# Two encoder layers on one core: raw blocks of the first product chunks fetched between the plain chunks, FFN forms made in one paced chain, a quarter of the plain weights' low halves by subtraction, activations' low halves on VectorE

## The chip, the cores and the metric

The kernel runs on one core of a Trainium2 chip. The metric is the device time of one execution in microseconds (us). The profile is of one execution; TensorE is PE in it, VectorE DVE, ScalarE ACT, GpSimd POOL, SyncE SP. A name such as L508 is line 508 of the kernel before.

## The reference, cut to what matters

Two layers, 512 tokens of 1024 channels, all in float32. Each layer has an attention part with three branches, which the change leaves alone, and a gated FFN:

```python
for l in range(DEPTH):                       # DEPTH = 2
    ...                                      # attention, pooling, gates, output projection
    hf = rms_norm(x, ffn_norm_g[l])
    u = depthwise_conv(hf @ ffn_w_up[l], ffn_conv_w[l], ffn_conv_b[l])   # 1024 -> 2*2816, width 3
    u_gate, u_val = u[..., :D_FF], u[..., D_FF:]
    x = x + (jax.nn.silu(u_gate) * u_val) @ ffn_w_down[l]                # 2816 -> 1024
```

## The kernel before

**Three matmuls for one.** A float32 product is made of three of a rounded type: each operand is split into a high half (its rounded value) and a low half (the rest), and hi·hi, hi·lo and lo·hi are summed. So every weight and every activation must be split before TensorE can use it. In the profile `wh`, `wl` are the halves of a weight, `HH`, `HL` those of the activations held in the long-lived buffers, `ah`, `al` those in short-lived ones.

**The FFN.** The 2816 hidden columns are 22 chunks of 128. A chunk has two parts, gate and value. Chunks 0 to 5 are **plain**: a part is eight steps of three matmuls of 128x512 into one PSUM tile (`ps_acc`, `ps_ST`, `ps_AV` in turn). Its weight comes in two pieces of 128x512, called units here, so that the plain stretch of a layer uses 24 units, numbered 0 to 23 in order of use, each 12 matmuls long. Chunks 6 to 21 are **product** chunks: gate and value come from seven products of 256 columns (`FORMS`), made from four raw blocks of 128x512 and sums of them, and from sums and differences of the normed input. The "down" projection (`ps_mi`) of finished chunks is dealt between the products.

**Plain weights.** SyncE fetches raw weights in one stream (`w_dma`, L390) into slots: three of 128x1024 (`RAW`) for two units each, and eight of 128x512 (`ALONE`) for the product chunks' blocks. A fetch is issued when a slot of its kind comes free (`w_free`), and the stream is strictly in order. `w_split` makes the halves of a unit. For a unit of kind "u", which all plain FFN units are, `by_transfer` (L414 to L423) has ScalarE write the high half, ScalarE write its negative into the low half, and GpSimd issue a DMA that adds the raw weight to it (L421); the row is `wl<-raw`, a DMA_DIRECT2D on POOL. For kind "p" it is a subtraction on VectorE or GpSimd, whichever a table of expected finish times calls sooner (`pick`). Product blocks' halves are `fh` and `fl`, by transfer, or come from sums on VectorE.

`wnext` is called where TensorE is about to use a unit, and has units split up to `LA` = 3 ahead, or `LAF` = 6 when the unit used now, or the one six on, belongs to a product.

**The forms.** When the normalising factor `rbc` is known, `build_forms` writes the normed input (`hn`, eight tiles), sums of its pieces (`tt`, four steps of four), and splits these into the product operands `tf`: names "11", "12" from `hn`, "1", "2", "22", "3" from `tt`, each a ScalarE copy and a VectorE subtraction. There are three chains of such steps, all started together. This runs beside the plain chunks. There VectorE also scales each finished part (`u`), convolves it (two SCALAR_TENSOR_TENSOR, `a<-u,prm,a`), and multiplies gate and value (`a<-a,a`); ScalarE then writes the product's high half, and GpSimd subtracts for the low half (`HL<-a,HH` or `al<-a,ah`, `eng=G` in `convolve`).

**The order.** A planner with a clock of its own records the program: `at` puts a step on its calendar, `chain` runs steps in turn, `need` marks what TensorE uses next. The engines then run what was recorded in order, each its own queue, so a step that waits holds up whatever was recorded behind it on the same engine.

Of the kernel before, what the change touches and what calls it, by code (L numbers as in the profile page):

```python
# [19 lines left out]
T = 512  # L20
D = 1024
KC = D // P
# [17 lines left out]
MID = 5  # L40
PRE_A = 16
PRE_B = 8
LA, LAF = 3, 6
SIZES = (6, 5, 4, 4, 3)
PLACE = {1: 0, 2: 5, 3: 0}
KEEP = 2
FORMS = ("11", "12", "1", "22", "2", "4", "3")
SPOTS = ("22", "2", "4", "3")
END = object()
# [83 lines left out]
def _layer_units():  # L133

    r = [("p", wd) for wd in _widths()]
    for tok in _ffn():
        if tok[0] == "u":
            r += [("u", T)] * 2
        elif tok[0] == "f":
            r.append(tok)  # L140
        elif (tok[2] * SIZES[tok[1]] + tok[3]) % 4 == 0:
            r.append(("u" if tok[1] < len(SIZES) - 1 else "p", T))
    return r


def _stream():


    pieces, slots, units, alone = [], [], [], []
    for kind, *u in _layer_units() * L:  # L150
        if kind == "f":
            if u[1] == FORMS[0]:
                first = len(pieces)
                for _ in range(4):
                    pieces.append((len(slots), 0, T))
                    slots.append(T)
                    alone.append(True)
            units.append((u[1], first))
            continue
        if len(slots) <= KC or alone[-1] or slots[-1] + u[0] > 1024:  # L160
            slots.append(0)
            alone.append(False)
        pieces.append((len(slots) - 1, slots[-1], u[0]))
        slots[-1] += u[0]
        units.append((kind, len(pieces) - 1))
    return pieces, slots, units, alone
# [25 lines left out]
class Clock:  # L192
# [37 lines left out]
    def done(self, *key):  # L230
        self.ready[key] = self.fin + self.SEM
# [7 lines left out]
    def has(self, *keys):  # L239
        return all(self.ready.get(k, 1e9) <= self.now for k in keys)  # L240

    def chain(self, *steps, after=0.2):

        def go(n, source=None):
            if n == len(steps):
                return
            keys, fn = steps[n] if isinstance(steps[n], tuple) else ((), steps[n])
            late = [self.ready.get(k, self.now + 0.5) for k in keys]
            if late and max(late) > self.now:
                self.at(max(late) - self.now, lambda: go(n))  # L250
                return
            self.fin, self.source, self.last = self.now, source, None
            fn()
            source, self.source = self.last, None
            self.at(max(0.0, self.fin - self.now), lambda: go(n + 1, source))
        self.at(after, lambda: go(0))

    def drain(self):
# [63 lines left out]
def trunk(ctx: ExitStack, tc: tile.TileContext, x, w, prm, gb, cst, out):  # L322
# [3 lines left out]
    at, need, done, chain = ck.at, ck.need, ck.done, ck.chain  # L326
    V, A, G = Engine(ck, nc.vector, "DVE"), Engine(ck, nc.scalar, "ACT"), Engine(ck, nc.gpsimd, "Pool")
# [48 lines left out]
    def f(ap):  # L376
        return ap.bitcast(F32)


    pieces, swidth, units, alone = _stream()  # L380
# [43 lines left out]
    def w_split():  # L424
        j = st["split"]
        kind, pi = units[j]
        st["split"] += 1
        if kind not in "pu":
            w_form(j, kind, pi)
            return  # L430
        sl, off, wd = pieces[pi]
        w_until(sl)
        r = raws[sl][:, off:off + wd]
        hi, lo = halves[j] = pair(j)
        ck.fin = ck.now
# [11 lines left out]
        if pi + 1 == len(pieces) or pieces[pi + 1][0] > sl:  # L447
            w_free(sl)

    def w_form(j, form, pi):  # L450
# [47 lines left out]

    def wnext():
        j = st["use"]  # L500
        n = LAF if any(units[min(i, len(units) - 1)][0] not in "pu" for i in (j, j + LAF)) else LA
        w_ahead(j + n if j > LA else j)
        st["use"] += 1
        need(("w", j))
        return halves.pop(j)
# [161 lines left out]
    def layer(l, sq, xsrc):  # L667
# [918 lines left out]
        act = {}  # L1586
# [8 lines left out]
        def build_forms():  # L1595
# [10 lines left out]
            def normed(k):  # L1606
                hn[k] = slot("hn")[:, :T]
                V.scalar_tensor_tensor(hn[k], XM[:, k, :], col(PRM_FG + k), fin["rbc"][:, :T], ALU.mult, ALU.mult)
                done("hn", l, k)

            def sums(q):
                a, b = hn[2 * q], hn[2 * q + 1]
                t = tt[q] = (slot("tt")[:, :T], slot("tt")[:, :T])
                V.tensor_tensor(t[0][:, lo], a[:, hi], a[:, lo], ALU.subtract)
                V.tensor_tensor(t[1][:, lo], b[:, hi], a[:, hi], ALU.subtract)
                V.tensor_tensor(t[0][:, hi], b[:, hi], t[0][:, lo], ALU.subtract)
                V.tensor_tensor(t[1][:, hi], b[:, lo], t[0][:, hi], ALU.subtract)
                done("tt", l, q)
# [36 lines left out]
        def convolve(c, part, u):  # L1655
            ci = c + part * FC
            a = slot("a")
            steps = [
                lambda: A.activation(a[:, :T], u[:, :T], AF.Identity, bias=col(PRM_B + ci),
                                     scale=col(PRM_W1 + ci)),  # L1660
                lambda: V.scalar_tensor_tensor(a[:, 1:T], u[:, 0:T - 1], col(PRM_W0 + ci), a[:, 1:T],
                                               ALU.mult, ALU.add),
                lambda: V.scalar_tensor_tensor(a[:, 0:T - 1], u[:, 1:T], col(PRM_W2 + ci), a[:, 0:T - 1],
                                               ALU.mult, ALU.add)]
            if part == 0:
                def gate():
# [340 lines left out]
```

## Time and profile before

| what | value |
|---|---|
| time, median of 3 runs | 1579.79 us (1577.57 to 1582.62) |
| the profiled execution's time | 1578.39 us |
| its span in the trace | 1576.6 us |
| its mean granted TensorE clock | 0.997 |
| plain stretch of layer 0, 432.65 to 498.00: VectorE busy | 50.51 of 65.35 us |
| the same: ScalarE busy | 50.44 us |
| the same: GpSimd busy, and its instructions | 32.08 us, 30 |
| the same: mean busy share of the DMA engines | 0.85 |

How to read the rows: a row of the timeline gives start, duration, engine, line, operation, output<-inputs, and in brackets the engine's idle time ahead of it with what ended it. A row of waits gives total, count and the longest. A row of windows gives a stretch, its length, the busy time of PE, weight loads, DVE, ACT and POOL with the number of instructions that started in it, then the granted TensorE clock, the DMA share and GB/s. TensorE's matmuls overlap, so the distance between starts is what one costs, and not the duration shown. A DMA_DIRECT2D row on POOL is the issue of a transfer; its landing is in the DMA view.

### The profile page before, as it was taken

How to read it: one execution, taken by the hardware profiler on the slowest of the kernel's cores; microseconds unless marked ns; L12 is line 12 of the kernel's file. 1: busy time of each engine (PE TensorE's matmuls, PEld its weight loads, DVE VectorE, ACT ScalarE, POOL GpSimd, SP SyncE). 2: the span in 40 equal slices, each digit the busy share in tenths (PEclk: the TensorE clock that was granted, in tenths of full speed). 3: DMA queues.
4: the chain of work that ended last, by engine and by line, in shares of the span. 5: the costliest groups of instructions: out<-in, count | busy, mean ns of one | idle time of the engine just before them, and what ended most of it. 6: DMA issues, size and time to landing. Idle time of an engine off the chain costs nothing.

```text
span 1576.6 us, 23997 instructions
## 1 busy us (share of the span) xinstructions
PE 1548.2 (98%) x8193; PEld 1338.6 (85%) x8193; DVE 1111.4 (70%) x1816; ACT 1034.4 (66%) x1932; POOL 859.7 (55%) x868
## 2 busy tenths in 40 slices
PE   9999989999999999999999999899999999999999
PEld 8888878888877999998888888788888779999987
DVE  6867886875278777777656688778652877777774
ACT  5557776763478777777655587666535787777773
POOL 3974876854653433333588658668546443333333
PEclk9999999999999999999999999999999999999999
DMA  5432224324489887886535322343244798888853
GB/s 205 126 114 74 74 85 144 107 67 134 113 179 230 200 193 185 205 183 132 135 117 141 100 74 74 96 138 101 70 146 123 170 229 192 192 198 187 194 113 101
DMA packets 127563, 222.36 MB, mean 141 GB/s; under 512 B 29648, under 2 KB 51664, under 8 KB 127440
## 3 DMA queue, kind: packets, MB, share of 16 engines
q1 hardware_dynamic: 90864, 162.93, 33.2%
q0 software_dynamic: 31680, 57.69, 21.3%
q8 instruction: 64, 1.05, 0.3%
q10 hardware_dynamic: 4896, 0.21, 0.2%
q14 instruction: 59, 0.48, 0.1%
HBM read 149.41 MB, written 13.63 MB: 103 GB/s over the span
## 4 chain that ended last, share of the span: by engine, by line
PE 74%; DVE 13%; ACT 6%; issue 4%; POOL 2%; DMA 1%; SPq 0%; ACTq 0%; DVEq 0%; POOLq 0%
PE ps_acc L508 32%; PE ps_AV L508 14%; PE ps_ST L508 12%; PE ps_S L508 8%; PE ps_mi L508 8%; DVE a L294 2%; DVE XM L290 2%; ACT wh L283 1%; DVE wl L290 1%; DVE u L290 1%; DVE mgl L290 1%; ACT mgh L283 1%; DVE hn L294 1%; ACT fh L283 1%; DVE tf L290 1%
## 5 line engine op out<-in xcount | busy, mean ns | idle before, releaser
L290 POOL TENSOR_TENSOR wl<-raw,wh 128x512 fp32r<-128x512 f32 (+3 forms) x241 | 305.0, 1275 | 224.6 <-ACT wh L283 206.5
L283 ACT ACTIVATE wh<-raw 128x512 fp32r<-128x512 f32 (+2 forms) x457 | 269.2, 605 | 56.9 <-DVE raw L290 12.9
L421 POOL DMA_DIRECT2D wl<-raw x124 | 110.9, 919 | 290.3 <-ACT wl L283 106.0
L508 PE MATMUL ps_acc<-HH,wl 128*128 128x512 f32 x416 | 164.3, 395 | 6.2 <-DMA wl<-raw 6.2
L508 PE MATMUL ps_acc<-HH,wh 128*128 128x512 f32 x416 | 164.1, 394 | 3.4 <-DVE vm L290 2.9
L294 DVE SCALAR_TENSOR_TENSOR a<-u,prm,a 128x511 f32<-128x511 f32 x176 | 142.8, 811 | 32.2 <-ACT a L283 31.2
L508 PE MATMUL ps_acc<-HL,wh 128*128 128x512 f32 x416 | 163.5, 393 | 0.0
L421 POOL DMA_DIRECT2D fl<-raw x96 | 85.2, 887 | 105.7 <-ACT sx L283 47.0
L290 DVE TENSOR_TENSOR wl<-raw,wh 128x512 fp32r<-128x512 f32 (+2 forms) x93 | 92.4, 995 | 60.6 <-ACT wh L283 60.5
L283 ACT ACTIVATE a<-u,prm 128x512 f32<-128x512 f32 x88 | 71.5, 815 | 86.6 <-DVE u L290 86.2
L298 DVE TENSOR_REDUCE nm<-ps_S 128x1 fp32r<-128x512 f32 x128 | 87.6, 685 | 36.0 <-PE ps_S L508 34.8
L508 PEld LDWEIGHTS ps_acc<-HH,wl 128*128 128x128 f32 x416 | 78.8, 189 | 24.9 <-DMA wl<-raw 7.9
L508 PEld LDWEIGHTS ps_acc<-HH,wh 128*128 128x128 f32 x416 | 79.0, 190 | 19.8 <-issue 4.4
L508 PE MATMUL ps_AV<-tf,wh 128*128 128x256 f32 x512 | 94.8, 283 | 0.0
L508 PE MATMUL ps_acc<-tf,wh 128*128 128x256 f32 x512 | 94.4, 282 | 0.0
L508 PE MATMUL ps_ST<-tf,fh 128*128 128x256 f32 x512 | 94.2, 281 | 0.0
L508 PEld LDWEIGHTS ps_acc<-HL,wh 128*128 128x128 f32 x416 | 78.9, 190 | 16.3
L508 PEld LDWEIGHTS ps_acc<-tf,wh 128*128 128x128 f32 x512 | 83.9, 191 | 5.3
L508 PEld LDWEIGHTS ps_AV<-tf,wh 128*128 128x128 f32 x512 | 81.4, 190 | 2.6
L283 ACT ACTIVATE wl<-wh 128x512 fp32r<-128x512 f32 x124 | 78.5, 633 | 3.9
L508 PEld LDWEIGHTS ps_ST<-tf,fh 128*128 128x128 f32 x512 | 79.4, 190 | 0.0
L508 PE MATMUL ps_acc<-tf,wl 128*128 128x256 f32 x256 | 72.4, 283 | 0.0
(417 smaller groups left out, 4844.8 us busy)
## 6 DMA issues: line engine op xcount, KB each, us to landing
raw<-w SPq DMA_DIRECT2D x162, 512.0 KB, 3.7
raw<-w SPq DMA_DIRECT2D x136, 256.0 KB, 4.2
wl<-raw POOLq DMA_DIRECT2D x124, 256.0 KB, 4.3
fl<-raw POOLq DMA_DIRECT2D x96, 256.0 KB, 5.4
raw<-w SPq DMA_DIRECT2D x14, 384.0 KB, 3.0
XM<-x SPq DMA_DIRECT2D x16, 256.0 KB, 3.2
dtq<-tr SPq DMA_DIRECT2D x16, 192.0 KB, 1.9
dtk<-tr SPq DMA_DIRECT2D x16, 192.0 KB, 2.0
```

What stands on the lines that cost most here:

```text
L283: return self.eng.activation(out, in_, func, **k)
L290: return self.eng.tensor_tensor(out, *a)
L294: return self.eng.scalar_tensor_tensor(out, *a)
L298: return self.eng.tensor_reduce(out, in_, *a, **k)
L421: nc.gpsimd.dma_start(f(lo), r, accum_op=ALU.add)
L508: PE.matmul(o, lhsT=lhsT, rhs=rhs, start=start, stop=stop, skip_group_check=again)
```

## The change

Five edits, all in the FFN:

1. **Fetch order.** After each of the last eight of the twelve plain parts, one raw block of the first two product chunks is put into the stream of fetches (the "q" marks), instead of four in a row ahead of each of these chunks.
2. **Low halves.** The second unit of each value part becomes kind "p": six of the 24 plain units of a layer (units 3, 7, 11, 15, 19, 23) are split by subtraction. `pick` gives all of them to GpSimd. This takes six ScalarE copies and six accumulating DMAs out of each layer.
3. **Lookahead** is `LAP` = 4 where plain units are in use.
4. **Forms.** `hn` and `tt` steps alternate in one chain that starts no step sooner than 0.9 us after the last, and all cuts stand in one chain with 0.8 us, where two chains without a pace were.
5. **Activations.** From chunk 5 on, the low halves of activations are subtracted on VectorE, 17 per layer.

```diff
-LA, LAF = 3, 6
+LA, LAP, LAF = 3, 4, 6
+PACE_H, PACE_F = 0.9, 0.8
...
         if tok[0] == "u":
-            r += [("u", T)] * 2
+            r += [("u", T), ("p" if tok[2] else "u", T)] + [("q",)]
...
+    early, plain, fresh = [], 0, False
     for kind, *u in _layer_units() * L:
+        if kind == "q":
+            plain = (plain + 1) % (2 * SIZES[0])
+            if plain and plain >= 2 * SIZES[0] - 8:
+                early.append(len(slots))
+                slots.append(T)
+                alone.append(True)
+            continue
...
                 for _ in range(4):
+                    if early:
+                        pieces.append((early.pop(0), 0, T))
+                        continue
...
-        if len(slots) <= KC or alone[-1] or slots[-1] + u[0] > 1024:
+        if len(slots) <= KC or fresh or alone[-1] or slots[-1] + u[0] > 1024:
...
-            self.at(max(0.0, self.fin - self.now), lambda: go(n + 1, source))
+            self.at(max(pace, self.fin - self.now), lambda: go(n + 1, source))
...
-        n = LAF if any(units[min(i, len(units) - 1)][0] not in "pu" for i in (j, j + LAF)) else LA
+        kinds_ = [units[min(j + i, len(units) - 1)][0] for i in (0, LAP, LAF)]
+        n = LAF if any(k not in "pu" for k in kinds_) else LAP if "u" in kinds_[:2] else LA
...
-            chain(*[lambda k=k: normed(k) for k in range(KC)], *[lambda q=q: sums(q) for q in range(4)], after=0.0)
-            for names in (("11", "1", "2"), ("12", "22", "3")):
-                chain(*[z for name in names for q in range(4) for z in cut(name, q)], after=0.3)
+            chain(*[z for q in range(4) for z in (lambda q=q: normed(2 * q), lambda q=q: normed(2 * q + 1), lambda q=q: sums(q))],
+                  after=0.0, pace=PACE_H)
+            chain(*[z for name in ("11", "12", "1", "2", "22", "3") for q in range(4) for z in cut(name, q)], after=0.3, pace=PACE_F)
...
-            return steps + [([("gate", l, c)], prod), *split(ah, al, a[:, :T], eng=G), lambda: done("act", l, c)]
+            return steps + [([("gate", l, c)], prod), *split(ah, al, a[:, :T], eng=G if c < SIZES[0] - 1 else V), lambda: done("act", l, c)]
```

How it moves instructions is shown at three places of layer 0; layer 1 has the same pattern. TensorE's order is the same in both kernels. The numbers behind a name only tell buffers apart, and the lines of the changed kernel lie 13 or 14 further down.

The first place is SyncE's queue in the second half of the plain stretch. Before:

```order
L390 DMA raw_4842<-w 128x1024
L390 DMA raw_4905<-w 128x1024
L390 DMA raw_4969<-w 128x1024
L390 DMA raw_5026<-w 128x1024
L390 DMA raw_5083<-w 128x1024
L390 DMA raw_5085<-w 128x512
L390 DMA raw_5087<-w 128x512
L390 DMA raw_5089<-w 128x512
L390 DMA raw_5091<-w 128x512
L390 DMA raw_5161<-w 128x1024
```

The last plain chunk's fetch, raw_5083, is followed by the four blocks of the first product chunk. In the changed kernel the queue reads, from the fetch for units 8 and 9:

```order
L403 DMA raw_4625<-w 128x1024
L403 DMA raw_4627<-w 128x512
L403 DMA raw_4679<-w 128x1024
L403 DMA raw_4681<-w 128x512
L403 DMA raw_4759<-w 128x1024
L403 DMA raw_4761<-w 128x512
L403 DMA raw_4817<-w 128x1024
L403 DMA raw_4819<-w 128x512
```

The blocks of 128x512 now stand one by one behind the fetches of 128x1024.

The second place is GpSimd's queue in the middle of the plain stretch, units 10 to 17. Before (L421 issues a transfer, L290 is a subtraction):

```order
L421 DMA wl_4797<-raw_4706 128x512
L421 DMA wl_4825<-raw_4706 128x512
L421 DMA wl_4853<-raw_4791 128x512
L421 DMA wl_4883<-raw_4791 128x512
L290 TENSOR_TENSOR al_4693<-a_4691,ah_4692 128x512
L421 DMA wl_4917<-raw_4842 128x512
L290 TENSOR_TENSOR al_4822<-a_4820,ah_4821 128x512
L421 DMA wl_4944<-raw_4842 128x512
L421 DMA wl_4981<-raw_4905 128x512
L421 DMA wl_5007<-raw_4905 128x512
```

In the changed kernel the same units read:

```order
L434 DMA wl_4782<-raw_4679 128x512
L303 TENSOR_TENSOR wl_4835<-raw_4679,wh_4834 128x512
L434 DMA wl_4839<-raw_4759 128x512
L434 DMA wl_4870<-raw_4759 128x512
L434 DMA wl_4899<-raw_4817 128x512
L303 TENSOR_TENSOR al_4700<-a_4698,ah_4699 128x512
L303 TENSOR_TENSOR al_4832<-a_4830,ah_4831 128x512
L303 TENSOR_TENSOR wl_4953<-raw_4817,wh_4952 128x512
L434 DMA wl_4957<-raw_4879 128x512
L434 DMA wl_4996<-raw_4879 128x512
```

Two of the transfers, for units 11 and 15, are now subtractions on GpSimd itself, and the two `al` stand together behind unit 14's transfer.

The third place is VectorE's queue at the end of chunk 18, where its activations are split. Before:

```order
L290 TENSOR_TENSOR u_7924<-ps_ST_7950,sx_7926 128x256
L290 TENSOR_TENSOR a_7913<-a_7913,a_7877 128x512
L290 TENSOR_TENSOR wl_7975<-s_1126_7895,wh_7974 128x512
L290 TENSOR_TENSOR raw_7775<-raw_7775,raw_7793 128x512
L290 TENSOR_TENSOR wl_8032<-raw_7775,wh_8031 128x512
L290 TENSOR_TENSOR XM<-ps_mi_8022,XM 128x512
```

In the changed kernel:

```order
L303 TENSOR_TENSOR u_7919<-ps_ST_7944,sx_7921 128x256
L303 TENSOR_TENSOR a_7908<-a_7908,a_7871 128x512
L303 TENSOR_TENSOR wl_7969<-s_1126_7888,wh_7968 128x512
L303 TENSOR_TENSOR HL<-a_7908,HH 128x512
L303 TENSOR_TENSOR raw_7763<-raw_7763,raw_7789 128x512
L303 TENSOR_TENSOR wl_8026<-raw_7763,wh_8025 128x512
L303 TENSOR_TENSOR XM<-ps_mi_8016,XM 128x512
```

`HL`, which GpSimd made between two transfer issues before, stands on VectorE behind the low half of a sum and ahead of the next sum of raw blocks.

More of the change, by code (lines that the diff above doesn't have):

```diff
@@ L149, in _stream @@
     pieces, slots, units, alone = [], [], [], []
+    early, plain, fresh = [], 0, False
     for kind, *u in _layer_units() * L:
+        if kind == "q":
[5 more added lines that the diff above has]
+            continue
         if kind == "f":
             if u[1] == FORMS[0]:
-                first = len(pieces)
+                first, fresh = len(pieces), True
                 for _ in range(4):
+                    if early:
+                        pieces.append((early.pop(0), 0, T))
+                        continue
                     pieces.append((len(slots), 0, T))
@@ L159, in _stream @@
             continue
-        if len(slots) <= KC or alone[-1] or slots[-1] + u[0] > 1024:
+        if len(slots) <= KC or fresh or alone[-1] or slots[-1] + u[0] > 1024:
             slots.append(0)
             alone.append(False)
+        fresh = False
         pieces.append((len(slots) - 1, slots[-1], u[0]))
@@ L240, in has, with chain @@
         return all(self.ready.get(k, 1e9) <= self.now for k in keys)
-    def chain(self, *steps, after=0.2):
+    def chain(self, *steps, after=0.2, pace=0.0):
         def go(n, source=None):
@@ L446, in w_split @@
         done("w", j)
-        if pi + 1 == len(pieces) or pieces[pi + 1][0] > sl:
+        if pi + 1 == len(pieces) or pieces[pi + 1][0] != sl:
             w_free(sl)
```

## The prediction, made blind

> **What bounds the kernel now.** I read the page's busy line and chain first, then TensorE's waits, its timeline at those waits, and last the queues that it waits for.
>
> ```profile
> span 1576.6 us, 23997 instructions
> ...
> PE 1548.2 (98%) x8193; PEld 1338.6 (85%) x8193; DVE 1111.4 (70%) x1816; ACT 1034.4 (66%) x1932; POOL 859.7 (55%) x868
> ...
> PE 74%; DVE 13%; ACT 6%; issue 4%; POOL 2%; DMA 1%; SPq 0%; ACTq 0%; DVEq 0%; POOLq 0%
> ```
>
> TensorE is busy 98% of the span, and the change leaves its instructions and their order alone. So it can only win or lose TensorE's waits. Those that touch the changed code, as total, count and longest, are:
>
> ```profile
> PE ps_acc L508 <- DMA wl<-raw: 6.2, 3, 3.0
> PE ps_mi L508 <- POOL HL L290: 4.6, 2, 2.4
> ...
> PE ps_ST L508 <- DMA wl<-raw: 1.6, 2, 0.9
> ```
>
> Five waits, 7.8 us, are for the accumulating transfer of a plain low half; two, 4.6 us, are for an activation's low half made on GpSimd. A wait costs more than its idle figure, as TensorE's timeline shows (start, duration, what, idle ahead of it):
>
> ```profile
> 466.65 0.50 PE L508 MATMUL ps_acc<-HH,wl 128*128 128x512 f32 x1 [0.70 <-DMA wl<-raw]
> ...
> 472.00 0.39 PE L508 MATMUL ps_ST<-HL,wh 128*128 128x512 f32 x1
> 473.09 0.50 PE L508 MATMUL ps_ST<-HH,wl 128*128 128x512 f32 x1 [0.70 <-DMA wl<-raw]
> 473.42 0.39 PE L508 MATMUL ps_ST<-HH,wh 128*128 128x512 f32 x1
> 473.65 0.39 PE L508 MATMUL ps_ST<-HL,wh 128*128 128x512 f32 x1
> ```
>
> Undisturbed, starts lie 0.23 apart (473.42 to 473.65) though a row lasts 0.39. From 472.00 to 473.09 are 1.09, so 0.86 is lost where 0.70 is shown, and the next start comes after 0.33, 0.10 late. Each wait costs about 0.27 above its figure. A long one also costs clock:
>
> ```profile
> 486.79 0.50 PE L508 MATMUL ps_acc<-HH,wl 128*128 128x512 f32 x1 [2.52 <-DMA wl<-raw]
> ...
> 1268.11 0.80 PE L508 MATMUL ps_acc<-HH,wl 128*128 128x512 f32 x1 [2.96 <-DMA wl<-raw]
> ...
> 1273.82 0.45 PE L508 MATMUL ps_acc<-HH,wh 128*128 128x512 f32 x1
> ...
> 1511.82 0.50 PE L508 MATMUL ps_mi<-HL,wh 128*128 128x512 f32 x1 [2.37 <-POOL HL L290]
> ```
>
> ```profile
> 1270.00:1275.00 5.00, 5.00 (x15) 3.94 (x14) 1.09 (x3) 4.91 (x11) 2.84 (x4) 0.61 1.07 240
> ...
> 1510.00:1515.00 5.00, 3.18 (x15) 3.00 (x16) 3.09 (x3) 1.43 (x4) 2.68 (x3) 0.79 1.00 222
> 1515.00:1520.00 5.00, 5.00 (x28) 4.35 (x27) 3.94 (x8) 3.42 (x6) 0.87 (x1) 0.87 0.30 52
> ```
>
> Thirteen pitches from 1268.11 to 1273.82 took 5.71 instead of 13 × 0.227 = 2.95: 2.8 lost at a clock of 0.61. After 1511.82 the two windows give 5 × 0.21 + 5 × 0.13 = 1.7. The wait of 2.52 at 486.79 dropped nothing.
>
> So the plain stretches lose 7.8 + 5 × 0.27 + 2.8 = **12.0**, the activation waits 4.6 + 2 × 0.27 + 1.7 = **6.8**. Of the profiled execution's 1578.4 us, 18.8 can go: the floor is 1559.6.
>
> **Activations' low halves to VectorE.** At the end of chunk 18 (the same in layer 1):
>
> ```profile
> 722.51 0.69 DVE L290 TENSOR_TENSOR wl<-s,wh 128x512 fp32r<-128x512 f32 x1
> ...
> 726.37 2.29 DVE L290 TENSOR_TENSOR wl<-raw,wh 128x512 fp32r<-128x512 f32 x1 [2.57 <-ACT wh L283]
> ```
>
> ```profile
> 723.74 0.62 ACT L283 ACTIVATE HH<-a 128x512 fp32r<-128x512 f32 x1
> ```
>
> ```profile
> 726.52 1.58 POOL L290 TENSOR_TENSOR HL<-a,HH 128x512 fp32r<-128x512 f32 x1
> ```
>
> ```profile
> 725.51 0.40 PE L508 MATMUL ps_mi<-HH,wh 128*128 128x512 f32 x1
> 728.15 0.50 PE L508 MATMUL ps_mi<-HL,wh 128*128 128x512 f32 x1 [2.25 <-POOL HL L290]
> ```
>
> HH is there at 724.36. GpSimd starts HL 2.2 later, behind a transfer's issue, and TensorE, ready for it at 725.51 + 0.23 = 725.74, starts it at 728.15. In the new order HL stands on VectorE right behind the wl<-s of 722.51: 724.4 + 0.69 = 725.1, 0.6 ahead of need. Both waits go: **−6.8**. Late next is the raw<-raw sum that now stands behind HL and its wait for HH: it ran at 723.11 and would end near 725.8. Its copy on ScalarE started at 725.72 anyhow, behind other copies, so this costs about 0.1, and the wl behind it, 2.29 beside GpSimd's HL, falls back to 0.69. The other moved halves add 17 × 0.69 = 11.7 us of VectorE per layer:
>
> ```profile
> 615.00:670.00 55.00, 55.00 (x372) 50.80 (x371) 39.60 (x64) 40.72 (x73) 19.53 (x21) 1.00 0.84 199
> ```
>
> VectorE is 72% busy there and TensorE waits for nothing; I price them at nothing. Without that cover, a VectorE held for HH would cost what the wait above costs GpSimd's reader, up to 2.4 at a chunk; the other end is a gain of nothing.
>
> **Fetches and lookahead.** What TensorE waits for is issued on GpSimd's queue:
>
> ```profile
> 460.66 0.87 POOL L421 DMA_DIRECT2D wl<-raw  x1 [2.05 <-ACT tf L283]
> ...
> 463.76 3.72 POOL L290 TENSOR_TENSOR al<-a,ah 128x512 fp32r<-128x512 f32 x1
> 467.43 0.86 POOL L421 DMA_DIRECT2D wl<-raw  x1
> ...
> 480.01 0.89 POOL L421 DMA_DIRECT2D wl<-raw  x1 [2.74 <-ACT tf L283]
> ```
>
> The DMA view gives the time to landing, in this order: for the issue at 460.66; at 467.43; and for the stretch 479.9 to 480.9 with SP's burst of five blocks:
>
> ```profile
> wl<-raw POOLq DMA_DIRECT2D x1, 256.0 KB, 5.9
> ```
>
> ```profile
> wl<-raw POOLq DMA_DIRECT2D x1, 256.0 KB, 5.6
> ```
>
> ```profile
> raw<-w SPq DMA_DIRECT2D x1, 512.0 KB, 4.3
> raw<-w SPq DMA_DIRECT2D x2, 256.0 KB, 5.7
> wl<-raw POOLq DMA_DIRECT2D x1, 256.0 KB, 6.7
> ```
>
> TensorE wanted them at landing less loss: 460.66 + 5.9 − 0.9 = 465.7, 5.0 after the issue; likewise 467.43 + 5.6 − 0.9, 4.7 after; and 480.01 + 6.7 − 2.7, 4.0 after. A lookahead of four units instead of three issues one unit earlier, and a unit is 12 matmuls, 12 × 0.227 = 2.7 us: 7.7, 7.4 and 6.7 of lead. With the fetches dealt one block to a part, I take the third landing as 5.7 like the others (bounds 3.3, the same transfer at 476.42 with no fetch beside it, and 6.7). Margins: 1.8, 1.8, **1.0**. With nothing else changed, all five waits end. SP works its queue in order, so a lone block without a slot would hold the next 128x1024 fetch back by up to one fetch, 4.3; there are eight such slots for eight blocks, and none is in use until the products, so 0 it is.
>
> **Subtractions and forms.** Six transfers of 24 become GpSimd subtractions; each saves an issue (0.87) and a ScalarE copy, but stands in GpSimd's row among the transfers, beside a VectorE that is full:
>
> ```profile
> 480.00:485.00 5.00, 4.27 (x19) 3.19 (x17) 5.00 (x10) 3.85 (x8) 3.07 (x3) 1.00 0.67 186
> ```
>
> ```profile
> 467.69 2.49 DVE L294 SCALAR_TENSOR_TENSOR a<-u,prm,a 128x511 f32<-128x511 f32 x1
> ...
> 472.76 0.74 DVE L294 SCALAR_TENSOR_TENSOR a<-u,prm,a 128x511 f32<-128x511 f32 x1
> ...
> 482.82 1.74 DVE L294 SCALAR_TENSOR_TENSOR a<-u,prm,a 128x511 f32<-128x511 f32 x1
> ...
> 496.76 1.78 DVE L294 SCALAR_TENSOR_TENSOR a<-u,prm,a 128x511 f32<-128x511 f32 x1
> ```
>
> Beside GpSimd's al at 468.05, 482.45 and 496.04 the same VectorE row grew by 1.75, 1.0 and 1.04; I take the mean, 1.26, for each. Three subtractions (units 7, 11, 15) stand ahead of the third wait: 3.8 us of slip against its margin of 1.0, hence 2.8 of stall if all of it reaches the weights' copies, 0 if none does. VectorE is what ScalarE's copies wait for, so I go near the upper end: 2 a layer, **4.0 left of the 12.0**. The forms' count is unchanged and their one paced chain only spreads them over the same full VectorE; 0, between −2 (the later forms then stop holding convolutions) and +2 (the last cut late at the first product).
>
> The Trainium skill ("TensorE: Matmul & The Clock Gate", What's actually happening) puts the drop after an idle window of about 3.4 us that runs free. By that, waits of 2 us cost no clock, which is the sum; but 2.37 was enough at 1511.82, so the measurement decides and a drop goes into the range.
>
> Sum on the profiled 1578.4: −6.8 − 8.0 = 1563.6. That execution is 1.4 under the median of 1579.79, so **1565.0**.
>
> **Rivals.**
> *All plain waits end.* The slip does not reach the copies, since the paced forms leave VectorE room: 1559.6 + 1.4 = 1561.0. For it: margins without slip are positive. Against: VectorE's 5.00 of 5.
> *The plain stretches don't improve.* Layer 0 loses 4.7 there now (0.70 + 0.70 + 2.52 + 3 × 0.27); 5.7 of slip against the margin of 1.0, 1.9 for each subtraction instead of 1.26, brings that back, and only the ends count: 1578.4 − 6.8 + 1.4 = 1573.0. For it: the 2.49 above is 1.75 of slip. One clock drop fewer or more moves it 2.8.
> *Slower: VectorE and GpSimd hold each other.* Al at 463.76 took 3.72 where its kind takes this when VectorE is quiet:
>
> ```profile
> 1284.94 1.32 POOL L290 TENSOR_TENSOR al<-a,ah 128x512 fp32r<-128x512 f32 x1 [4.44 <-ACT ah L283]
> ```
>
> If each of the five subtractions in the form stretch (units 7 to 23) costs that on the path, for the 0.87 of an issue: 5 × 2.85 = 14.3, less 1.0 of margin 13.3 of stall, and 2.8 of clock, 16.1 a layer. That is 32.2 where the forecast leaves 4.0: 1565.0 + 28.2 = 1593.2. It decides from 7.6 of slip a layer, 1.5 for each, since then 2 × (6.6 + 2.8) eats the 18.8.
> On this the Trainium skill ("SBUF — State Buffer", Who interferes with whom) speaks against the change: a VectorE instruction with two SBUF inputs and a GpSimd one that reads SBUF contend, for a port pair that is locked exclusively. The 3.72 and 2.49 agree; by its "whole instruction" each meeting costs at most the other's own length, 1.32, which would make the slip 4.0 rather than 3.8 and the time 1565.4.
>
> **How the numbers follow.** Forecast (1562.5 to 1569, with a clock drop at one stall): 0.48. All waits end (1559 to 1562): 0.20. Only the ends (1571 to 1574.5): 0.15. Nothing seen, the moved halves costing what they save: 0.07. Slower: 0.10. The range 1558.5 to 1574.5 holds the first three, 0.83. A measurement of this kernel tells apart about 0.3%, 4.7 us; so faster 0.82, same 0.08, slower 0.10.
>
> **What would show it.** The two POOL HL waits must be gone and the clock at 1.00 near the end of chunk 18 in both layers; if TensorE waits there for VectorE's HL, that step is wrong. Waits for wl should be about 2 us a layer; none means the first rival, the old 7.8 the second. Lookahead: issue to need about 7 instead of 4 to 5 us; fetches: no transfer over 6 in the plain stretch. Subtractions: VectorE rows beside them near 1.9, not over 3; GpSimd's near 1.5, not 3.7. A new wait for a form (tf) at the first products would break the price of nothing for the chain.

## The result, and the profile after

| | before | after |
|---|---|---|
| median of 12 runs | 1578.74 us (1574.97 to 1582.68) | 1581.60 us (1579.27 to 1584.85) |
| profiled execution (span) | 1578.39 (1576.6) | 1579.78 (1578.0) |
| start of layer 0's FFN, 2001st to 2401st matmul | 80.73 | 85.70 |
| the same in layer 1, 6001st to 6401st | 90.36 | 93.96 |
| end of layer 0's products, 3601st to 4001st | 60.91 | 58.39 |
| the same in layer 1, 7601st to 8001st | 62.11 | 57.91 |

The ratio is 1.0016, 95% interval 1.0004 to 1.0028: slower by 2.5 us, within the 0.3% that was called the same, where 1565.0 was forecast. The last four rows are times between starts of TensorE's matmuls, whose order both kernels share, so a stretch can be compared directly. The two ends gained 2.52 + 4.20 = 6.7 us together; the two FFN starts lost 4.97 + 3.60 = 8.6. Elsewhere the two traces agree within 0.6 in a stretch of 400 matmuls.

The page after, with busy times and the chain:

```profile
span 1578.0 us, 23956 instructions
...
PE 1551.6 (98%) x8193; PEld 1342.0 (85%) x8193; DVE 1108.8 (70%) x1850; ACT 1027.2 (65%) x1920; POOL 815.7 (52%) x834
...
PE 82%; DVE 7%; ACT 4%; issue 3%; POOL 2%; DMA 1%; SPq 0%; ACTq 0%; DVEq 0%; POOLq 0%
```

The shares of DVE, ACT and POOL in the chain fell from 21% to 13%, and yet the time rose: the chain's shares say who ended last, not how long. TensorE's waits after:

```profile
PE ps_ST L522 <- DVE tf L303: 4.7, 4, 2.2
PE ps_ST L522 <- DMA wl<-raw: 4.3, 2, 2.4
...
PE ps_AV L522 <- DMA wl<-raw: 2.1, 2, 1.1
...
PE ps_ST L522 <- ACT tf L296: 0.4, 2, 0.2
PE ps_ST L522 <- DMA fl<-raw: 0.3, 1, 0.3
```

The POOL HL waits are gone. Four waits for plain low halves remain, 6.4 us against 7.8. New are the waits at the first products, nearly all for `tf`, the forms: 4.7 + 0.4 + 0.3 = 5.4 us. On TensorE's timeline:

```profile
491.48 0.50 PE L522 MATMUL ps_ST<-HH,wl 128*128 128x512 f32 x1 [2.39 <-DMA wl<-raw]
...
492.57 0.63 PE L522 MATMUL ps_ST<-HH,wl 128*128 128x512 f32 x1
492.99 0.63 PE L522 MATMUL ps_ST<-HH,wh 128*128 128x512 f32 x1
...
509.38 0.39 PE L522 MATMUL ps_ST<-tf,fh 128*128 128x256 f32 x1 [0.83 <-DVE tf L303]
...
512.07 0.39 PE L522 MATMUL ps_ST<-tf,fh 128*128 128x256 f32 x1 [0.92 <-DVE tf L303]
...
1292.68 0.38 PE L522 MATMUL ps_ST<-tf,fh 128*128 128x256 f32 x1 [2.25 <-DVE tf L303]
```

Behind the wait of 2.39 starts lie 0.42 apart, not 0.23: the clock dropped again. Two windows of layer 0 show what was granted:

```profile
490.00:500.00 10.00, 8.53 (x30) 6.89 (x31) 6.77 (x10) 7.72 (x16) 5.21 (x5) 0.83 0.89 174
...
510.00:520.00 10.00, 8.93 (x44) 7.64 (x45) 8.22 (x16) 9.03 (x21) 2.63 (x3) 0.83 0.48 104
```

Each lost 10 × 0.17 = 1.7 us to the clock. In both FFN starts together the clock stood at half for 6.8 us before and for 13.6 after. So the 8.6 are made up of 4.0 more waits (11.8 against 7.8), up to 3.4 for the lower clock, and what each of the added waits costs beside its figure.

Why the forms are late shows on VectorE. The last cut of layer 0 before, and then three rows after: a convolution step, the cut of form 22 for which TensorE waits at 512.07, and the last cut:

```profile
498.46 0.41 DVE L290 TENSOR_TENSOR tf<-tt,tf 128x256 fp32r<-128x256 f32 x1
```

```profile
493.73 2.88 DVE L307 SCALAR_TENSOR_TENSOR a<-u,prm,a 128x511 f32<-128x511 f32 x1 [3.16 <-ACT a L296]
...
511.60 0.42 DVE L303 TENSOR_TENSOR tf<-tt,tf 128x256 fp32r<-128x256 f32 x1
...
520.63 0.43 DVE L303 TENSOR_TENSOR tf<-tt,tf 128x256 fp32r<-128x256 f32 x1 [0.44 <-ACT tf L296]
```

The cut that is waited for ends at 512.02, 13 us after all cuts were done before (498.87). The factor `rbc` was ready at 447.20 before and 448.28 after, so the last cut came 51.7 us behind it before and 72.8 after. The windows between factor and last cut, before and after:

```profile
447.20:498.87 51.67, 47.75 (x208) 38.58 (x207) 47.41 (x85) 43.66 (x81) 23.83 (x23) 1.00 0.85 193
```

```profile
448.28:521.06 72.78, 67.37 (x311) 55.50 (x310) 63.67 (x101) 52.70 (x99) 28.49 (x28) 0.95 0.73 165
```

VectorE (the third busy time) was idle 51.67 − 47.41 = 4.3 us in the first, 9.1 in the second. It stood idle while cuts were still owed. Each of the longer gaps ended with a ScalarE step: 4.2 us for `a`, a convolution's first step, 3.1 for the copies of forms, 1.2 for an activation's high half. The longest, 3.16 ahead of 493.73, waited for an `a` that ScalarE had recorded behind halves of the first products' weights:

```profile
492.36 0.63 ACT L296 ACTIVATE fl<-fh 128x512 fp32r<-128x512 f32 x1
492.90 0.80 ACT L296 ACTIVATE a<-u,prm 128x512 f32<-128x512 f32 x1
```

### The profile page after: what moved, and what is told of

It reads as the page before. It is cut to its first block, busy times and chain, and to the rows that moved or that the text cites. A ratio compares the mean times of both kernels' runs of the same rounds, so it can differ in the third digit from the quotient of the medians.

```text
span 1578.0 us, 23956 instructions
## 1 busy us (share of the span) xinstructions
PE 1551.6 (98%) x8193; PEld 1342.0 (85%) x8193; DVE 1108.8 (70%) x1850; ACT 1027.2 (65%) x1920; POOL 815.7 (52%) x834
## 4 chain that ended last, share of the span: by engine, by line
PE 82%; DVE 7%; ACT 4%; issue 3%; POOL 2%; DMA 1%; SPq 0%; ACTq 0%; DVEq 0%; POOLq 0%
PE ps_acc L522 34%; PE ps_AV L522 16%; PE ps_ST L522 13%; PE ps_mi L522 10%; PE ps_S L522 10%; DVE a L307 1%; DVE XM L303 1%; ACT wh L296 1%; DMA wl<-raw 1%; DVE mgl L303 1%; ACT mgh L296 1%; ACT a L296 0%; DVE gt L307 0%; DVE sq L303 0%; ACT wl L296 0%
## 5 line engine op out<-in xcount | busy, mean ns | idle before, releaser
L303 POOL TENSOR_TENSOR wl<-raw,wh 128x512 fp32r<-128x512 f32 (+3 forms) x253 | 321.6, 1280 | 244.0 <-ACT wh L296 216.6
L434 POOL DMA_DIRECT2D wl<-raw x112 | 99.0, 888 | 288.5 <-ACT sx L296 123.7
L307 DVE SCALAR_TENSOR_TENSOR a<-u,prm,a 128x511 f32<-128x511 f32 x176 | 146.6, 834 | 32.7 <-ACT a L296 31.0
L303 DVE TENSOR_TENSOR wl<-raw,wh 128x512 fp32r<-128x512 f32 (+2 forms) x93 | 68.7, 739 | 43.1 <-ACT wh L296 42.8
L296 ACT ACTIVATE wl<-wh 128x512 fp32r<-128x512 f32 x112 | 70.9, 633 | 3.6
L522 PE MATMUL ps_ST<-tf,fl 128*128 128x256 f32 x256 | 72.8, 284 | 0.3 <-DMA fl<-raw 0.3
```

What stands on the lines that cost most here:

```text
L296: return self.eng.activation(out, in_, func, **k)
L303: return self.eng.tensor_tensor(out, *a)
L307: return self.eng.scalar_tensor_tensor(out, *a)
L434: nc.gpsimd.dma_start(f(lo), r, accum_op=ALU.add)
L522: PE.matmul(o, lhsT=lhsT, rhs=rhs, start=start, stop=stop, skip_group_check=again)
```

## The experiments

Edits are numbered as in the section on the change. "FFN starts" is the sum of the two FFN-start stretches, as in the table above; before it is 171.1, after 179.7. It is free of the rest of the kernel, but from one execution each: it holds the chance of a clock drop, and a drop of 3.4 us at half clock is worth 1.7, so differences under 2 us are not read as effects.

The ratio is to the kernel before, run beside each kernel; its median there was 1577.35 to 1579.19 us. Between runs of different rows, differences in us are therefore worked out from the ratios, as a share of 1579. The planner records anew when an edit changes its steps, so most of these kernels differ in their order at more places than the edit. The runs with less or more VectorE work keep the order, two places on VectorE apart in b5_light and two on ScalarE in b5_heavy; a_sub_twice and a_sub_memset only add to GpSimd's queue.

| run | what | ratio to before | FFN starts, us |
|---|---|---|---|
| b_acts_dve | 5 | 0.9960 (0.9947 to 0.9973) | 169.9 |
| b_form_chain | 4 | 1.0017 (1.0007 to 1.0026) | 174.7 |
| b_look_acts | 3, 5 | 0.9939 (0.9925 to 0.9953) | 166.7 |
| b_fetch_acts | 1, 5 | 0.9945 (0.9932 to 0.9959) | 168.2 |
| b_fetch_look_acts | 1, 3, 5 | 0.9961 (0.9948 to 0.9975) | 167.4 |
| a_no_form_chain | 1, 2, 3, 5 | 0.9954 (0.9941 to 0.9966) | 168.0 |
| a_no_subtract | 1, 3, 4, 5 | 0.9967 (0.9956 to 0.9978) | 171.2 |
| a_chain_order | all, form 22 cut ahead of 2 | 1.0033 (1.0023 to 1.0044) | 180.5 |
| a_chain_unpaced | all, paces 0 | 1.0008 (0.9996 to 1.0019) | 177.7 |
| a_sub_on_dve | all, subtractions on VectorE | 1.0034 (1.0022 to 1.0047) | 181.2 |
| b5_light | 5, less VectorE work | 0.9920 (0.9893 to 0.9947) | 164.2 |
| a_light | all, less VectorE work | 0.9937 (0.9916 to 0.9959) | 167.7 |
| b135_light | 1, 3, 5, less VectorE work | 0.9892 (0.9866 to 0.9918) | 160.8 |
| b5_heavy | 5, more VectorE work | 1.0045 (1.0032 to 1.0059) | 183.4 |
| b135_tf12 | 1, 3, 5, form 12's low by transfer | 0.9994 (0.9983 to 1.0006) | 175.0 |
| b135_tf1112 | the same for 11 and 12 | 1.0034 (1.0021 to 1.0046) | 182.7 |
| a_sub_twice | all, subtractions doubled | 1.0058 (1.0044 to 1.0071) | 185.2 |
| a_sub_memset | all, memsets behind them | 1.0053 (1.0041 to 1.0066) | 176.6 |

**Edit 5 alone** (against before):

```diff
-*split(ah, al, a[:, :T], eng=G)
+*split(ah, al, a[:, :T], eng=G if c < SIZES[0] - 1 else V)
```

> The kernel before with edit 5 alone (activations' low halves from chunk 5 on VectorE). Theory A (the moved halves gain what the two waits cost, and the late forms ate it in the changed kernel): both POOL HL waits gone, about 6.8 us less than before, ratio 0.9957. Rival B (the gain comes back later as VectorE's own lateness): waits gone but the ratio 0.999 to 1.002, with new waits on DVE in the product stage.

1572.45 against 1579.04: 6.6 us less, and no wait for HL. Theory A: the forecast's first term stands.

**Without the form chain** (against after; the old three chains are put back):

```diff
-            chain(*[z for name in ("11", "12", "1", "2", "22", "3") for q in range(4) for z in cut(name, q)], after=0.3, pace=PACE_F)
+            for names in (("11", "1", "2"), ("12", "22", "3")):
+                chain(*[z for name in names for q in range(4) for z in cut(name, q)], after=0.3)
```

> The changed kernel with edit 4 undone (forms in three unpaced chains as before, everything else kept). Theory A (the single paced chain puts the cuts of forms 22 and 3 too late): the eight waits for tf at the first products go, with the clock drop after them, 8 to 10 us less than the changed kernel, ratio to before 0.994 to 0.996. Rival B (the subtractions on GpSimd slow VectorE, and forms are late whatever their chain): tf waits stay, ratio 1.000 to 1.003.

0.9954 against 1.0016: 9.8 us less than the changed kernel, and no wait for tf. VectorE between factor and last cut:

```profile
449.25:500.35 51.10, 48.64 (x212) 39.35 (x212) 50.68 (x84) 40.80 (x77) 23.74 (x22) 1.00 0.83 185
```

It idles 0.4 of 51.1 us there, and the last cut comes as soon behind the factor as before, subtractions and all. Theory A, near its upper number.

**Without the subtractions** (against after):

```diff
-            r += [("u", T), ("p" if tok[2] else "u", T)] + [("q",)]
+            r += [("u", T), ("u", T)] + [("q",)]
```

> The changed kernel with edit 2 undone (all 24 plain low halves by transfer). Theory A: tf waits stay near 5 us, ratio 0.999 to 1.003. Rival B (subtractions make VectorE late): tf waits go, wl waits shrink, ratio 0.994 to 0.997.

0.9967, 7.7 us less. Here theory A fails: its range gave at most 4. Rival B has the ratio and the shrinking waits for wl, but not the rest of its picture, since tf waits stay:

```profile
PE ps_ST L522 <- DVE tf L303: 3.9, 8, 1.0
...
PE ps_AV L522 <- DMA wl<-raw: 0.8, 2, 0.5
```

The plain stretch is all but free of waits. Undoing either edit gives most of the loss back, 9.8 or 7.7 us. Together that is more than the changed kernel lost at its FFN starts (8.6), so their costs are not separate terms.

**The form chain alone** (against before; the diff above reversed, with the `hn` and `tt` chain):

> The kernel before with edit 4 alone (one paced chain of forms). Theory A: tf waits appear at the first products in both layers, 3 to 5 us a layer with the clock, ratio 1.003 to 1.006. Rival B: no tf waits, ratio 0.998 to 1.001.

1581.60 against 1579.04, 2.6 more: between the ranges of theory A and rival B. Waits appear as theory A says, smaller, and the waits for wl grow from 7.8 to 8.6:

```profile
PE ps_acc L521 <- DMA wl<-raw: 7.2, 2, 3.9
...
PE ps_ST L521 <- ACT tf L296: 1.7, 2, 1.0
...
PE ps_AV L521 <- DMA wl<-raw: 1.4, 2, 0.7
PE ps_ST L521 <- DVE tf L303: 1.1, 3, 0.4
```

In FFN starts the chain costs 3.6 alone (174.7 − 171.1), 3.8 beside edits 1, 3 and 5 without subtractions (171.2 − 167.4) and 11.7 with them (179.7 − 168.0). The subtractions cost 0.6 without the chain (168.0 − 167.4), which is nothing that this measure can tell, and 8.4 with it.

**Edits 1, 3 and 5** (against after: both diffs above):

> The kernel before with edits 1, 3 and 5 (the changed kernel without its subtractions and without its form chain). Theory A (subtractions and chain each cost, the other three edits gain about 11 of the 12.0 and all of the 6.8): wl waits under 2 us in all, no tf waits, 1578.9 - 17 = 1562, ratio 0.988 to 0.991. Rival B (with three unpaced chains the plain waits come back, since VectorE is full again): wl waits of 3 to 6 us, ratio 0.994 to 0.997.

0.9961 (1571.91 us), no less than edit 5 alone with 0.9960. All waits for wl in the plain stretch are gone, and this is what came instead, at the first products:

```profile
PE ps_ST L522 <- DMA fl<-raw: 4.3, 3, 1.6
...
PE ps_mi L522 <- DMA wl<-raw: 2.3, 2, 2.0
```

Theory A is refuted on this term. Rival B has the ratio, but not the picture: the time comes back one stage later. Some of it lies behind the FFN start: the 400 matmuls that follow it in layer 1 take 61.03 us against 58.51 before, so that the 167.4 of the table is too good by 2.5. The plain stretch did what was forecast, and the kernel gained nothing by it.

**The subtractions on VectorE** (against after; kind "pu" is "p" with the engine fixed):

```diff
-            e = V if j < KC + 3 else pick(W_BIAS, ck.fin + ck.SEM)
+            e = V if j < KC + 3 or kind == "pu" else pick(W_BIAS, ck.fin + ck.SEM)
```

> The changed kernel with its six subtractions a layer on VectorE instead of GpSimd. Theory L (they cost by standing in GpSimd's queue and by clashing with VectorE): at 0.69 each on VectorE the wl waits fall well below the changed kernel's 6.4 us, ratio 0.997 to 1.000. Theory D (any added time on the way costs, VectorE being full): wl and tf waits as long as in the changed kernel or longer, ratio 1.001 to 1.006.

1.0034. No wait for wl is left, as theory L says, but the time is theory D's: two waits, one a layer, take the place of all others. That of layer 0 ends at 512.99, while ScalarE makes five copies of forms in a row:

```profile
PE ps_ST L522 <- ACT tf L296: 18.2, 2, 9.1
```

```profile
512.53 1.63 ACT L296 ACTIVATE tf<-tt 128x256 fp32r<-128x256 f32 x5
```

They had been recorded behind the first products' weights. The planner recorded much of VectorE's and ScalarE's order anew in this run, and TensorE's at eight matmuls at the start of each FFN. So it doesn't tell VectorE's added time from the new order, and neither theory is shown.

**The chain's order, and its pace** (each against after):

```diff
-("11", "12", "1", "2", "22", "3")
+("11", "12", "1", "22", "2", "3")
```

```diff
-PACE_H, PACE_F = 0.9, 0.8
+PACE_H, PACE_F = 0.0, 0.0
```

> The changed kernel with the cuts of form 22 ahead of those of form 2 in its one chain, as the products use them. Theory O (the order of the cuts makes 22 late): tf waits of product 22 (on ps_ST) go, about 5 us with the clock, ratio 0.997 to 1.000. Theory P (the pace makes the whole tail late): waits stay over 3 us, on ps_ST or for form 2 on the next product, ratio 1.000 to 1.002.

> The changed kernel with both paces of its form chains at 0, the order kept. Theory P: tf waits go, ratio 0.995 to 0.998. Theory O: tf waits stay near 5 us, ratio 1.000 to 1.002.

With form 22 earlier, the tf waits go and 6.5 us for a ScalarE copy stand where the next product begins:

```profile
PE ps_acc L522 <- ACT sx L296: 6.5, 2, 3.3
PE ps_ST L522 <- DMA wl<-raw: 4.5, 2, 2.3
```

FFN starts 180.5 against 179.7: moved, not gained, and the ratio of 1.0033 lies above both theories' ranges. Without paces the tf waits fall to 1.0 us, as P says, but FFN starts are 177.7 and the ratio is 1.0008 (0.9996 to 1.0019) beside 1.0016, in O's range: waits for `sx` (3.2 us) stand in their place, and those for wl are 7.3 us where the changed kernel has 6.4. So neither the order nor the pace carries the cost by itself. What is left of edit 4 is the single chain of cuts, where two ran side by side, and `hn` and `tt` in turns; no run tells these two apart.

By now the theory was **W**: VectorE's work between factor and first products sets TensorE's loss, and a wait taken away in the plain stretch returns at the products. Three runs take work away and one adds some, with the recorded order kept:

```diff
-                lambda: V.scalar_tensor_tensor(a[:, 0:T - 1], u[:, 1:T], col(PRM_W2 + ci), a[:, 0:T - 1], ALU.mult, ALU.add)]
+                lambda: tap2(c, a, u, ci)]      # n = 16 columns if c < SIZES[0] else T - 1
```

```diff
+                nc.vector.tensor_tensor(u[:, :T], acc, fin["rbc"][:, :T], ALU.mult)
                 V.tensor_tensor(u[:, :T], acc, fin["rbc"][:, :T], ALU.mult)
```

> The kernel before with edit 5, and the second convolution tap of the plain chunks done on 16 of its 511 columns only (part of the result is left out), recorded in the same order: 12 x 0.6 = 7 us less VectorE work in each layer's plain stretch. Theory W (VectorE's work between the factor and the first products sets TensorE's loss; a wait taken away in the plain stretch comes back at the first products): 8 to 11 us less than edit 5 alone, ratio to before 0.989 to 0.991. Theory Q (the waits come from places in queues and from transfers): 0 to 3 less, ratio 0.994 to 0.996.

> The changed kernel with the same taps cut to 16 columns, order kept (part of the result is left out). Theory W: of its 21 us of loss at the two FFN starts 12 to 14 go, ratio 0.992 to 0.995. Theory Q: waits for wl and tf stay within 2 us, ratio 1.000 to 1.003.

> Before with edits 1, 3 and 5 and the same taps cut (part of the result is left out). Theory W: the waits for fl and wl at the first products go, 8 to 11 less than 1571.9, ratio 0.989 to 0.992, as for edit 5 alone with the cut taps. Theory Q: the waits stay, ratio 0.994 to 0.996.

> Before with edit 5, the scaling u of each plain part done twice on VectorE (12 x 0.6 = 7.2 us more work a layer, same result). Theory W: 11 to 14 us more than edit 5 alone, ratio 1.003 to 1.005. Theory Q: 0 to 4 more, ratio 0.996 to 0.999.

A shortened tap takes 0.23 where the whole one takes 0.75, so that 24 of them take about 12 us away over both layers, not 14. By the ratios the changed kernel falls by 12.5, edits 1, 3 and 5 by 10.9, and 24 added rows of 0.60 from start to start, 14.4 us, cost 13.4: theory W in all three. In b5_heavy they show as waits for wl in the plain stretch (16.7 us where b_acts_dve has 7.8), with 6.8 us at half clock in each layer where b_acts_dve has 3.4 in one. Edit 5 alone falls by 6.3 only, short of W's 8 and above its range of ratios: with lookahead three and bursts of fetches, 3.6 us of waits for wl remain. So edits 1 and 3 are worth 4.5 us there (1567.52 − 1563.00), but only once VectorE is relieved.

**Lookahead and fetches apart** (against edits 1, 3, 5: the "q" marks out, or the old line in `wnext`):

> Before with edits 3 and 5 alone (lookahead four, fetches in the old order). If the lookahead is what ended the plain waits: waits for wl in the plain stretches under 1 us, and the loss at the first products as in edits 1, 3 and 5 together, ratio 0.995 to 0.997. If the fetches are: plain waits for wl of 3 us or more stay, ratio again 0.995 to 0.997, since by theory W the total hardly changes.

> Before with edits 1 and 5 alone (fetches between the plain chunks, lookahead three). If the fetches are what ended the plain waits: wl waits in the plain stretches under 1 us and waits at the first products; if the lookahead is, plain waits of 3 us or more stay. Ratio 0.995 to 0.997 either way by theory W.

Neither ends the plain waits by itself: 2.6 us for wl remain with the lookahead, 7.3 with the fetches. The ratios 0.9939 and 0.9945 are a little below what was expected and below the 0.9960 of edit 5 alone and the 0.9961 of both edits, by 2 to 3 us; but the intervals still overlap, in part barely (0.9925 to 0.9953 and 0.9948 to 0.9975). Whether either edit gains by itself stays open. b_look_acts has the lowest median of the kernels that compute everything, 1568.76.

**Real work off VectorE** (against edits 1, 3, 5):

```diff
+                if name in ("12",):             # or ("11", "12")
+                    def both():
+                        by_transfer(dh, dl, src())
+                        done("tf", l, name, q)
...
+                    return [([key], both)]
```

> Before with edits 1, 3 and 5, and the low halves of form 12 made like a weight's (ScalarE copy of the negative, accumulating transfer) instead of on VectorE: 4 x 0.68 = 2.7 us less VectorE work a layer, 4 ScalarE copies and 4 transfer issues more. Theory W (VectorE's work before the first products sets the loss, 1.2 to 2 us per us over both layers by the runs with cut and doubled work): 3 to 5 us less than 1571.9, ratio 0.993 to 0.995. Rival T (GpSimd's queue and the transfers set it): same or 1 to 3 us more, ratio 0.996 to 0.998.

> The same for the low halves of forms 11 and 12: 4 x 0.41 + 4 x 0.68 = 4.4 us less VectorE work a layer, 8 more transfers. Theory W: 4 to 7 us less than 1571.9, ratio 0.992 to 0.994. Rival T: same or up to 6 us more, ratio 0.996 to 1.000.

By the ratios 5.2 and 11.5 more, where W wanted 3 to 7 less: W as the only bound is refuted. The loss is above rival T's ranges, too. The waits are for wl again. Ahead of the longest of layer 0, b135_tf12 shows this on GpSimd and then on ScalarE:

```profile
473.35 1.57 POOL L434 DMA_DIRECT2D tf<-hn  x1
477.62 0.92 POOL L434 DMA_DIRECT2D wl<-raw  x1 [2.70 <-ACT tf L296]
```

```profile
475.51 0.63 ACT L296 ACTIVATE wh<-raw 128x512 fp32r<-128x512 f32 x1 [3.36 <-PE ps_ST L522]
```

```profile
PE ps_AV L522 <- DMA wl<-raw: 6.7, 2, 3.4
...
PE ps_ST L522 <- DMA wl<-raw: 1.6, 2, 1.2
```

GpSimd stood idle for 2.70 ahead of the weight's issue and waited for ScalarE, which had itself been idle for 3.36. So the row does not show the new issues holding up the weights. The run shows that work taken off VectorE and given to ScalarE, GpSimd and the DMA cost more than it saved; which of the three carries it stays open.

**What a subtraction costs on GpSimd** (each against after, behind or ahead of the line shown):

```diff
+                e.eng.tensor_tensor(lo[:, :wd], r, f(hi[:, :wd]), ALU.subtract)   # a_sub_twice
             e.tensor_tensor(lo[:, :wd], r, f(hi[:, :wd]), ALU.subtract)
+                for _ in range(12):                                               # a_sub_memset
+                    e.eng.memset(junk[:, :], 0.0)
```

> The changed kernel with each of its six subtractions a layer done twice on GpSimd (same result, 1.3 us more of GpSimd each). Undoing the subtractions took 8.1 us off. Theory L (a GpSimd operation that reads SBUF costs VectorE its time, and that is what hurts): 6 to 10 more than the changed kernel's 1.0016, ratio 1.0055 to 1.008. Theory N (their time does not matter, their place in the queue does): within 2 us of it, ratio 1.000 to 1.003.

> The changed kernel with twelve small memsets on GpSimd behind each of the six subtractions, about 1.2 to 1.5 us in all, which read nothing. Theory L: nearly free, ratio 1.000 to 1.003, clearly below the kernel with the subtractions doubled. Theory Q (GpSimd's time itself, ahead of the transfers in its queue, is what hurts): as much as the doubled subtractions, ratio 1.005 to 1.008.

Doubled, the kernel takes 6.6 us more (0.0042 of the ratio) and FFN starts rise by 5.5 (185.2), as theory L says. With memsets, which take longer on GpSimd, FFN starts fall by 3.1 (176.6); but the ratio, 1.0053, is the one that theory Q gave. In the doubled kernel, GpSimd and VectorE at the second subtraction of unit 11:

```profile
459.02 1.63 POOL L303 TENSOR_TENSOR wl<-raw,wh 128x512 fp32r<-128x512 f32 x1
```

```profile
459.41 1.79 DVE L307 SCALAR_TENSOR_TENSOR hn<-XM,prm,rbc 128x512 f32<-128x512 f32 x1
```

And in the kernel with memsets:

```profile
463.16 2.13 POOL L461 MEMSET junk<- 128x32 f32 x12
```

```profile
463.69 0.74 DVE L307 SCALAR_TENSOR_TENSOR hn<-XM,prm,rbc 128x512 f32<-128x512 f32 x1
```

The same VectorE operation takes 1.79 beside the subtraction and 0.74 beside memsets, and it is not the only one. Of the `hn` rows and convolution steps, all 14 that overlap memsets take 0.74 or 0.75; of the 19 that overlap a GpSimd subtraction in the changed kernel, 12 take 1.27 to 2.88. By "SBUF — State Buffer" of the Trainium skill (Who interferes with whom), a VectorE instruction with two SBUF inputs contends with a GpSimd one that reads SBUF, and not with one that only writes it. These rows agree.

The total time of the memset kernel doesn't decide between L and Q: its attention stretches are longer by 0.4 to 2 us per 400 matmuls as well (88.7 against 88.0 in the second), which the edit was not meant to touch. The edit also adds a tile to the kernel's memory; why the stretches grow stays open.

## Why the prediction was wrong, point by point

- **What bounds the kernel: right as reading, wrong as sum.** The losses were there (12.0 and 6.8). One step that failed is the floor of 1559.6 and what was drawn from it: each plain wait was a term to be struck out, and what is late next was asked only within the plain stretch. In b_fetch_look_acts the 7.8 us of plain waits went, 6.6 us (4.3 + 2.3) came up at the first products, and the ratio stayed that of edit 5 alone.
- **Activations' low halves: right.** −6.8 forecast, 6.7 in the two end stretches, 6.6 alone. VectorE is held 1.14 us for HH, the risk that was named, but HL ends at 728.65 and TensorE takes it up at 730.70: a margin of 2.0 and not 0.6, in layer 1 as well.

```profile
726.14 0.68 DVE L303 TENSOR_TENSOR wl<-s,wh 128x512 fp32r<-128x512 f32 x1
727.96 0.69 DVE L303 TENSOR_TENSOR HL<-a,HH 128x512 fp32r<-128x512 f32 x1 [1.14 <-ACT HH L296]
```

```profile
730.70 0.39 PE L522 MATMUL ps_mi<-HL,wh 128*128 128x512 f32 x1
```

- **Fetches and lookahead: right for the stretch.** No plain wait is left in b_fetch_look_acts, as "all five waits end" said. In the changed kernel they stay because units 16 and 20 are held up. For unit 16, GpSimd waits for an activation's high half, then subtracts, then issues; the transfer takes 6.4, over the 6 that was to be the limit:

```profile
468.61 1.42 POOL L303 TENSOR_TENSOR al<-a,ah 128x512 fp32r<-128x512 f32 x1 [3.16 <-ACT ah L296]
469.98 1.47 POOL L303 TENSOR_TENSOR wl<-raw,wh 128x512 fp32r<-128x512 f32 x1
471.40 0.89 POOL L434 DMA_DIRECT2D wl<-raw  x1
```

```profile
wl<-raw POOLq DMA_DIRECT2D x1, 256.0 KB, 6.4
```

- **Subtractions: the mechanism right, the size half.** 1.26 of slip each was taken for those ahead of the third wait. Unit 7's meets VectorE's step on the way to the factor, which takes 1.26 where it took 0.17 before, and so every form starts 1.1 later; that such a step could be met was not in the prediction:

```profile
446.20 0.17 DVE L290 TENSOR_TENSOR fac<-fac,C 128x16 f32<-128x16 f32 x1 [3.06 <-POOL fac L290]
```

```profile
446.13 1.28 POOL L303 TENSOR_TENSOR wl<-raw,wh 128x512 fp32r<-128x512 f32 x1
```

```profile
446.19 1.26 DVE L303 TENSOR_TENSOR fac<-fac,C 128x16 f32<-128x16 f32 x1 [3.06 <-POOL fac L303]
```

  Beside unit 11's, a convolution step takes 1.27 instead of 0.74. Beside unit 15's and the `al` ahead of it, two `tt` rows that take 0.87 take 2.94, 2.1 more:

```profile
468.80 2.94 DVE L303 TENSOR_TENSOR tt<-hn,tt 128x256 f32<-128x256 f32 x2
```

  2 us a layer were forecast; undoing them gives 4.2 a layer in FFN starts (8.4). That is with the form chain; without it they cost nothing that can be told, which no term of the sum could say.
- **Forms: the step that failed most.** They were priced at "0, between −2 and +2", on the ground that one paced chain "only spreads them over the same full VectorE". With it the last cut comes 21 us later behind the factor and VectorE idles 9.1 us instead of 4.3; undoing it gives 9.8 us, and alone it costs 2.6. A late cut at the first product was thought of, as the bound of +2 and as a last sign of being wrong, but it was priced for the chain alone and is not among the rivals.
- **Rivals.** "The plain stretches don't improve" (1573.0) had the plain part nearly right, 6.4 us of waits for 7.8, and lacked the new ones. The slower rival had the direction, but its lock of 3.72 didn't come: GpSimd's subtractions took 1.28 to 1.6. "Nothing seen" comes nearest to the measured time, but by luck: the moved halves saved their 6.7, and something else cost it again.

The cause, as far as the runs carry it: between the factor and the first products VectorE, ScalarE and GpSimd, each in its order, do a fixed amount of work for which TensorE waits somewhere. Shown is that VectorE's time counts nearly one for one there (b5_heavy, a_light, b135_light), that waits move rather than go (b_fetch_look_acts, a_chain_order), that VectorE is not the only bound (b135_tf12), and that the form chain and the subtractions cost their 8 to 12 us only together (a_no_form_chain, a_no_subtract). Not shown is why only together. A reading that fits the windows above is that the old chains leave VectorE 0.4 of idle time and absorb the slower rows, while the single chain passes the delay on to the products; it was not tried by itself.

## What to carry to other kernels

Before a wait is counted as gain, ask which engine worked through it: if it was full, the work is late at the next place that needs it, and the gain is what that engine saves, not what TensorE waited. Spreading work with a pace is not neutral when queues are in order: look where the last piece lands and whether its engine idles while pieces are owed. Try one edit alone and one edit undone; where the two disagree, as for the subtractions (0.6 or 8.4 us), the terms of a sum are not separate.

## What the hardware showed that was not expected

A wait of 2.39 us (491.48) halved TensorE's clock for some 3 us, as one of 2.37 did before, while one of 2.52 had not. Two waits of 0.83 and 0.92 (509.38 and 512.07) were followed by the same drop (0.83 in 510 to 520), so the length of the last wait alone doesn't tell. A GpSimd subtraction lengthened VectorE's rows by up to 2.1 us (2.88 instead of 0.74 at 493.73, beside an `al` of 1.96), which is more than the 1.32 that the prediction took as the most for one meeting, while twelve memsets of 2.13 us in all left them unchanged. Issuing an accumulating transfer of 128x2x256 took GpSimd 1.2 to 1.6 us where the 128x512 one takes 0.86.
